# Moving streamed rows to other places modulo 512 bytes in an fp32 encoder layer

## The chip, the cores and the metric

The kernel runs on one core of a Trainium2 chip. The metric is the device time of one execution in microseconds; a kernel's time is the median of its runs.

## What is computed

One encoder layer with two independent inputs of 1024 tokens and width 1024, in fp32: a normalised input is projected; one part goes through a gated long convolution by Fourier transforms (Hyena), one through attention in a window of 128; both are gated, merged and added to the input; then a gated feed-forward part with 2816 hidden columns.

```python
h = rmsnorm(x, norm1_g)
proj = h @ w_in
u_h, q, k, v, g_h, g_a = jnp.split(proj, splits, axis=-1)
y_h = hyena_mixer(u_h, short_w, short_b, filt, hyena_bias)
y_a = window_attention(partial_rope(q, pos), partial_rope(k, pos), v, sink_logit)
merged = sigmoid(g_h) * (y_h @ w_up_hyena) + sigmoid(g_a) * (y_a @ w_up_attn)
x = x + merged @ w_out
h = rmsnorm(x, norm2_g)
x = x + (silu(h @ w_ff_gate) * (h @ w_ff_up)) @ w_ff_down
```

## The kernel before, in words

Activations lie with features on the 128 partitions and tokens along the row, so a tile of [128, 1024] fp32 is a row of 4096 bytes in each partition. To reach fp32 precision, each large product is made of three matmuls in the type fp32r: every operand is split into a high part (a cast on ScalarE) and a low rest (a subtraction on VectorE), and high x high, high x low and low x high are added up in PSUM. In each matmul one operand is loaded as weights (128 columns, 512 bytes a partition) and the other, the right-hand side, is streamed past it (mostly 512 columns, 2048 bytes).

The tiles that matter here:

- whi and wlo, split weights (pool wp, left side), loaded as weights in every large product but those for q, k and v.
- hh0 to hh7 and hl0 to hl7, the high and low rows of the normalised input (pool pa). They are streamed in the projections for the convolution (gemm_rows, L584 to L586) and for the gates (L570 to L572), and loaded as weights in the projection for q, k and v (L778 to L780, 256 columns streamed from whi and wlo). Those hl rows whose slots were taken before by x0, the raw input, lie with it.
- yh, yl and mh, ml, the split rows of the merge (pools ya and ma), streamed at L570 to L572 too.
- r, a ring of 28 tiles that hold a high and a low row each, streamed in the feed-forward part, which uses Strassen's scheme (L1061 to L1063 up, L1258 to L1260 down). 21 of them are in the pool ra on the right side of SBUF, 7 in the pool ff on the left. GpSimd's queue fills them from DRAM (sides_in, L1040).
- the right side also holds, at other times, the tiles of the filters, the convolution and the attention.

SBUF is handed out in units of 32 bytes from both sides: pools on the left in the order in which they are opened, those with side="right" from the top downward. Tiles of the large pools are multiples of 512 bytes, so the place of a pool modulo 512 is the place of all its rows, and column slices of 128 or 512 fp32 keep it. Three tiles called gap, which nothing reads, set these places: one of 120 fp32 at the top of the right side, one of 8 at the bottom of the left side, and one of 32 in the pool pb, below ya, ma and ff. With them all the rows named above begin at 0 modulo 512. Two tiles in pb, s and xin, begin at 384.

The order of instructions is the order in which the Python code is written, with convolution and attention mixed into the projections by a table of rates; each engine runs its own list, and waits on the others by semaphores.

Of the kernel before, what the change touches and what calls it, by code (L numbers as in the profile page):

```python
# [11 lines left out]
F32 = mybir.dt.float32  # L12
F32R = mybir.dt.float32r
# [6 lines left out]
P = 128  # L20
T = 1024
# [91 lines left out]
class Ops:  # L113
    def __init__(self, tc):
        self.tc = tc
        self.nc = tc.nc
# [101 lines left out]
class Kern:  # L218
    def __init__(self, ctx, tc, a):
        self.ctx, self.tc, self.nc, self.a = ctx, tc, tc.nc, a  # L220
        self.sm = ctx.enter_context(tc.tile_pool(name="sm", bufs=1, space=PSUM))
        self.dr = ctx.enter_context(tc.tile_pool(name="dr", bufs=1, space=DRAM))
        self.cp = cp = ctx.enter_context(tc.tile_pool(name="cp", bufs=1))
        edge = ctx.enter_context(tc.tile_pool(name="edge", bufs=1, side="right"))
        self.nc.vector.memset(edge.tile([P, 120], F32, name="gap"), 0.0)
        self.nc.vector.memset(cp.tile([P, 8], F32, name="gap"), 0.0)
        self.gn = cp.tile([P, 3, KC], F32, name="gn")
        self.sw = cp.tile([P, 4, 12], F32, name="sw")
        self.eps = cp.tile([P, 1], F32, name="eps")
        self.sink = cp.tile([P, NQ], F32, name="sink")  # L230
        self.ident = self.cp.tile([P, P], F32, name="ident")
        make_identity(self.nc, self.ident)
        self.rates = RATES
        self.sas = itertools.cycle(("sa", "sd"))
        self.full = set()

    def psm(self, tag="sa"):
        if tag == "sa":
            tag = next(self.sas)
        return self.sm.tile([P, 512], F32, tag=tag, name=tag)  # L240
# [400 lines left out]
            nc.vector.tensor_tensor(acc[:, s], acc[:, s], sq, ALU.add)  # L641

    def h_tiles(self, hp, k):
        return [hp.tile([P, T], F32R, tag=f"h{e}{k}", name=f"h{e}{k}", bufs=1) for e in "hl"]


    def norm_stats(self, pool, src):
# [55 lines left out]
            self.nc.sync.dma_start(self.hn[k], x)  # L703

    def next_rows(self, pool):
        hs = []
        ws = [self.weights(self.a["w_u"][j], 8, P) for j in range(2)]
        for k in range(KC):
            x = pool.tile([P, T], F32, tag="t4", name="xin")
            self.nc.sync.dma_start(x, self.hn[k])  # L710
            hi, lo = self.h_tiles(pool, k)
            for s in HALVES:
                self.part(hi[:, s], lo[:, s], x[:, s])
            hs.append((hi, lo))
        todo = [(w, s, self.pmm()) for w, s in ((ws[0], HALVES[0]), (ws[1], HALVES[0]), (ws[0], HALVES[1]))]
        for _ in self.gemm_rows(todo, hs):
            pass
        self.late = lambda: self.gemm_one(ws[1], hs, HALVES[1])
        return hs, [todo[0][2], todo[2][2], todo[1][2]]
# [591 lines left out]
    def main(self, outs):  # L1311
        nc, tc = self.nc, self.tc
        self.setup()

        def drain(g):
            for _ in g:
                pass

        def mix(main, side, rate):

            t = 0.0
            for c in main:
                t += c * rate
                while side is not None and t > 0:
                    d = next(side, None)
                    if d is None:
                        side = None
                    else:
                        t -= d
            return side  # L1330
# [6 lines left out]
        def slow(g, f):  # L1337
            for c in g:
                yield c * f

        def chain(*gs):
            for g in gs:
                if g is not None:
                    yield from g
# [4 lines left out]
        with tc.tile_pool(name="pa", bufs=PA, reuse_waits="tile") as pool:  # L1349
            hs, early = self.first_rows(pool, xT[0])  # L1350
# [6 lines left out]
            hs, early = self.next_rows(pool)  # L1357
# [5 lines left out]
        with tc.tile_pool(name="pb", bufs=TB, reuse_waits="tile") as tmp:  # L1363
            acc = [None, None]
            hb = [{}, {}]
            rr = [None, None]
            with tc.tile_pool(name="ya", bufs=1, reuse_waits="tile") as yp, tc.tile_pool(name="ma", bufs=1, reuse_waits="tile") as pool:
                mr, ms = {}, {}

                def hyena_up(u):  # L1370
                    mr[u] = [yp.tile([P, 512], F32, tag=f"x{j}", name=f"x{j}") for j in range(8)]
                    yield from self.merge_up(u // 2, 0, mr[u], None, yp, pool, tmp, HALVES[u % 2])

                def attn_up(u):
                    ms[u] = []
                    yield from self.merge_up(u // 2, 1, mr[u], ms[u], yp, pool, tmp, HALVES[u % 2])

                def outp(u):
                    if u % 2 == 0:
                        acc[u // 2] = tmp.tile([P, T], F32, tag="ar", name="acc", bufs=self.arb)  # L1380
                    yield from self.merge_out(u // 2, ms[u], tmp, acc[u // 2], HALVES[u % 2])

                side = mix(chain(hyena_up(0), attn_up(0), hyena_up(1), outp(0), attn_up(1), hyena_up(2), outp(1)), side, R[6])
                if side:
                    drain(side)
                self.ra = self.ctx.enter_context(tc.tile_pool(name="ra", bufs=1, side="right", reuse_waits="tile"))

                def start(s):
                    rr[s] = self.norm_scale(tmp, acc[s])

                def first_b():
                    start(0)
                    rr[0] = self.spread_dma(tmp, rr[0])
                    yield 8
                    for k in range(3):
                        yield from self.b_side(tmp, 0, k, rr[0], hb[0])
                    two = [tmp.tile([P, 512], F32R, tag=YR[0], name="b11", bufs=YR[1]) for _ in range(2)]
                    self.b3 = self.b_side(tmp, 0, 3, rr[0], hb[0], two)
                    yield next(self.b3)

                side = mix(chain(slow(attn_up(2), UPW), slow(hyena_up(3), UPW), outp(2), slow(attn_up(3), UPW), outp(3)), first_b(), R[7])
                if side:
                    drain(side)
            with tc.tile_pool(name="ff", bufs=1, reuse_waits="tile") as fp:
                self.fp = fp
                nc.vector.memset(tmp.tile([P, 32], F32, tag="gap", name="gap", bufs=1), 0.0)
                self.stages = itertools.cycle(range(3))
                self.turn = itertools.cycle((None, "sa", None, "sb", "sa", None, "sc"))
                drain(self.b3)
                front = [None, None]  # L1410

                def load_front(s, pairs):
                    front[s] = (pairs, self.plain_acts(s, pairs, self.ring_tiles()))

                def scale_1():
                    start(1)
                    rr[1] = self.spread_dma(tmp, rr[1])

                def side_1(k):
                    t = fp.tile([P, 2, 2, 512], F32, tag="x3", name="xin", bufs=1)  # L1420
                    self.scaled(1, k, rr[1], (t[:, 0], t[:, 1]))
                    self.sides_out(t[:, 0], t[:, 1], self.bs[k])

                def squares():
                    acc = tmp.tile([P, T], F32, tag="ar", name="acc", bufs=self.arb)
                    for j in range(8):
                        self.square_sum(tmp, acc, x1[j], j == 0)
                    self.rf = self.final_scale(acc, tmp, slice(0, T))

                hooks = {2 * k + 1: lambda k=k: side_1(k) for k in range(4)}  # L1430
                self.ffn_up(0, hb[0], tmp, {0: scale_1, **hooks}, lambda: load_front(0, (0, 1)))
                x1, hb[1] = self.ffn_down(0, front[0], tmp, None, lambda: self.sides_in(self.bs))
                self.ffn_up(1, hb[1], tmp, {0: squares, 1: lambda: drain(self.finish(x1, self.rf, outs[0], slice(0, T)))}, lambda: load_front(1, (0,)))
                self.ffn_down(1, front[1], tmp, outs[1], lambda: None)
# [55 lines left out]
```

## Time and profile before

| | |
|---|---|
| median of 3 runs | 2923.15 us (2921.74 to 2924.38) |
| the profiled execution | 2927.37 us, span 2925.6 us |
| granted TensorE clock, mean | 0.989 |
| instructions | 36421 |
| DMA | 510.90 MB, mean 175 GB/s |

The profile's page gives each engine's busy time and share of the span; the timeline gives the start and the duration of single instructions; groups by line give the count, the busy time, the mean duration and the idle time before them with what ended it. PE is TensorE, PEld its weight loads, DVE VectorE, ACT ScalarE, POOL GpSimd. The time from one matmul's start to the next one's is called a step below.

### The profile page before, as it was taken

Reading aid. Unit: us, or ns where it says so; the run is one execution under the profiler, and the core shown is the slowest. Engines: PE = TensorE matmul, PEld = TensorE weight load, DVE = VectorE, ACT = ScalarE, POOL = GpSimd, SP = SyncE. Lnnn points to the kernel's source line nnn. Section 1 sums busy time; section 2 is a strip of 40 time slices with the busy share of each in tenths; the row PEclk is TensorE's granted clock in tenths of the full one; section 3 lists DMA queues with packets and bytes.
Section 4 is the critical chain, followed back from the end, with each engine's and each line's share of the span. In section 5 each row is a group of like instructions: output and inputs, shape, how many; then the busy total and the mean of one; then the engine's idle time right before and its main releaser. Section 6 shows DMA issues by size and latency. Waiting matters only on the chain.

```text
span 2925.6 us, 36421 instructions
## 1 busy us (share of the span) xinstructions
PE 2850.6 (97%) x13498; PEld 2340.6 (80%) x13498; DVE 2113.9 (72%) x3440; ACT 1231.9 (42%) x2040; POOL 74.9 (3%) x146
## 2 busy tenths in 40 slices
PE   8999799999999999999999999999999999999998
PEld 6789687877798778778887788888888888888887
DVE  6876799887766886796587667776555767766566
ACT  5344322267722324895454434444112434443122
POOL 0000000000000000000000000000122000001200
PEclk9999899999999999999999999999999999999999
DMA  4454665432263433446766345556666334447641
GB/s 160 145 206 169 229 218 180 145 125 67 67 199 117 160 118 120 142 137 190 228 225 201 128 153 201 204 217 243 268 247 256 131 128 158 159 158 290 268 158 68
DMA packets 202429, 510.90 MB, mean 175 GB/s; under 512 B 19623, under 2 KB 68427, under 8 KB 202253
## 3 DMA queue, kind: packets, MB, share of 16 engines
q1 hardware_dynamic: 182093, 435.18, 43.4%
q0 software_dynamic: 20160, 73.41, 6.3%
q8 instruction: 106, 1.74, 0.2%
q14 instruction: 70, 0.57, 0.1%
HBM read 350.69 MB, written 157.83 MB: 174 GB/s over the span
## 4 chain that ended last, share of the span: by engine, by line
PE 82%; DVE 8%; DMA 5%; ACT 4%; issue 1%; SPq 0%; DVEq 0%; ACTq 0%
PE mm L570 7%; PE mm L571 7%; PE mm L572 7%; PE mm L1061 4%; PE mm L1062 4%; PE mm L1063 4%; PE sc L403 2%; DMA gin<-gt 2%; PE mm L1260 2%; PE mm L1259 2%; PE mm L1258 2%; PE sb L1061 1%; PE sb L1063 1%; PE sc L1062 1%; PE sb L1062 1%
## 5 line engine op out<-in xcount | busy, mean ns | idle before, releaser
L348 ACT CAST whi<-raw 128x1024 fp32r<-128x1024 f32 (+1 forms) x270 | 264.9, 981 | 582.6 <-PE mm L571 208.7
L349 DVE TENSOR_TENSOR wlo<-raw,whi 128x1024 fp32r<-128x1024 f32 (+1 forms) x270 | 306.2, 1135 | 203.5 <-ACT whi L348 203.0
L570 PE MATMUL mm<-hh,whi 128*128 128x512 f32 x824 | 334.2, 406 | 12.1 <-DVE ge L797 12.1
L571 PE MATMUL mm<-hl,whi 128*128 128x512 f32 x824 | 334.4, 406 | 0.0
L572 PE MATMUL mm<-hh,wlo 128*128 128x512 f32 x824 | 333.3, 405 | 0.0
L348 ACT CAST whi<-s 128x1024 fp32r<-128x1024 f32 x104 | 109.1, 1049 | 243.6 <-PE mm L1062 57.0
L1062 PE MATMUL mm<-r,whi 128*128 128x512 f32 x518 | 201.8, 390 | 0.0
L1061 PE MATMUL mm<-r,whi 128*128 128x512 f32 x518 | 201.8, 390 | 0.0
L1063 PE MATMUL mm<-r,wlo 128*128 128x512 f32 x518 | 201.6, 389 | 0.0
L570 PEld LDWEIGHTS mm<-hh,whi 128*128 128x128 f32 x824 | 155.6, 189 | 40.6 <-DVE ge L797 12.6
L572 PEld LDWEIGHTS mm<-hh,wlo 128*128 128x128 f32 x824 | 155.4, 189 | 28.7 <-issue 0.5
L571 PEld LDWEIGHTS mm<-hl,whi 128*128 128x128 f32 x824 | 155.7, 189 | 28.4 <-issue 0.7
L349 DVE TENSOR_TENSOR wlo<-s,whi 128x1024 fp32r<-128x1024 f32 x104 | 127.1, 1222 | 15.9 <-ACT whi L348 15.4
L1040 POOL DMA_DIRECT2D r<-comb x112 | 59.4, 530 | 2650.8 <-PE mm L1063 2034.9
L1061 PEld LDWEIGHTS mm<-r,whi 128*128 128x128 f32 x518 | 97.4, 188 | 20.9 <-ACT c L1122 0.4
L1063 PEld LDWEIGHTS mm<-r,wlo 128*128 128x128 f32 x518 | 97.4, 188 | 20.6 <-DVE wlo L349 0.3
L1062 PEld LDWEIGHTS mm<-r,whi 128*128 128x128 f32 x518 | 97.4, 188 | 20.2
L778 PE MATMUL mm<-whi,hh 128*128 128x256 f32 x384 | 112.1, 294 | 0.0
L779 PE MATMUL mm<-wlo,hh 128*128 128x256 f32 x384 | 111.7, 292 | 0.0
L780 PE MATMUL mm<-whi,hl 128*128 128x256 f32 x384 | 110.6, 288 | 0.0
L570 PE MATMUL mm<-yh,whi 128*128 128x512 f32 x256 | 102.1, 402 | 5.2 <-DVE gin L938 3.9
L571 PE MATMUL mm<-yl,whi 128*128 128x512 f32 x256 | 102.1, 401 | 1.0 <-DVE yl L349 1.0
(586 smaller groups left out, 7270.3 us busy)
## 6 DMA issues: line engine op xcount, KB each, us to landing
r<-comb POOLq DMA_DIRECT2D x112, 512.0 KB, 9.6
comb<-stage SPq DMA_DIRECT2D x48, 1024.0 KB, 5.0
K<-kd SPq DMA_DIRECT2D x64, 384.0 KB, 3.4
raw<-in_w_fg SPq DMA_DIRECT2D x44, 512.0 KB, 5.5
raw<-in_w_fu SPq DMA_DIRECT2D x44, 512.0 KB, 3.8
raw<-in_w_g SPq DMA_DIRECT2D x32, 512.0 KB, 4.0
gt<-ge SPq DMA_DIRECT2D x32, 512.0 KB, 2.6
raw<-in_w_up SPq DMA_DIRECT2D x32, 512.0 KB, 4.2
```

Source lines behind the costliest of these rows:

```text
L348: self.nc.scalar.copy(hi, src)
L349: self.nc.vector.tensor_tensor(lo, src, hi.bitcast(F32), ALU.subtract)
L570: mm(ps, hi[:, k], xh[:, s], start=(i == 0), stop=False)
L571: mm(ps, hi[:, k], xl[:, s], start=False, stop=False)
L572: mm(ps, lo[:, k], xh[:, s], start=False, stop=(i == n - 1))
L778: nc.tensor.matmul(ps[:, q], xh[:, t], wh, start=(i == 0), stop=False)
L779: nc.tensor.matmul(ps[:, q], xh[:, t], wl, start=False, stop=False)
L780: nc.tensor.matmul(ps[:, q], xl[:, t], wh, start=False, stop=(i == 7))
L1040: self.nc.gpsimd.dma_start(t.bitcast(F32), src[q][PLACE[name]])
L1061: mm(ps, hi[:, k], xh, start=(first and k == 0), stop=False, skip_group_check=not first)
L1062: mm(ps, hi[:, k], xl, start=False, stop=False, skip_group_check=not first)
L1063: mm(ps, lo[:, k], xh, start=False, stop=(k == n - 1), skip_group_check=not first)
```

## The change

The gap tile on the right shrinks from 480 to 416 bytes, the one in pb grows from 128 to 160, and after each of the first six pairs of h tiles stands a new gap tile of 32 bytes, in the first input's pass only (the second one uses the same slots).

```diff
-        self.nc.vector.memset(edge.tile([P, 120], F32, name="gap"), 0.0)
+        self.nc.vector.memset(edge.tile([P, 104], F32, name="gap"), 0.0)
         self.nc.vector.memset(cp.tile([P, 8], F32, name="gap"), 0.0)
...
+        self.pad = True
...
     def h_tiles(self, hp, k):
-        return [hp.tile([P, T], F32R, tag=f"h{e}{k}", name=f"h{e}{k}", bufs=1) for e in "hl"]
+        hs = [hp.tile([P, T], F32R, tag=f"h{e}{k}", name=f"h{e}{k}", bufs=1) for e in "hl"]
+        if self.pad and k < 6:
+            self.nc.vector.memset(hp.tile([P, 8], F32, tag=f"gap{k}", name="gap", bufs=1), 0.0)
+        return hs
...
     def next_rows(self, pool):
+        self.pad = False
...
-                nc.vector.memset(tmp.tile([P, 32], F32, tag="gap", name="gap", bufs=1), 0.0)
+                nc.vector.memset(tmp.tile([P, 40], F32, tag="gap", name="gap", bufs=1), 0.0)
```

Worked out from the allocation, the places modulo 512 bytes are:

| rows | before | after |
|---|---|---|
| weights whi, wlo | 0 | 0 |
| hl0 to hl7, hh0 | 0 | 0 |
| hh1, hh2, hh3, hh4, hh5, hh6, hh7 | 0 | 32, 64, 96, 128, 160, 192, 192 |
| yh, yl, mh, ml | 0 | 32 |
| r in ff (7 tiles), and the other tiles of ff | 0 | 32 |
| r in ra (21 tiles) | 0 | 64 |
| filters, convolution, attention (right side) | 0 | 64 |

On TensorE, ScalarE, GpSimd and SyncE the instructions and their order are the same as before. Only VectorE's list changes, at its start. These are its first rows before:

```order
L225 MEMSET gap 128x120
L226 MEMSET gap 128x8
L508 MEMSET onef 128x128
L518 MEMSET eps 128x1
L262 MEMSET w_490 66x128
```

and here the same place after the change:

```order
L225 MEMSET gap 128x104
L226 MEMSET gap 128x8
L509 MEMSET onef 128x128
L647 MEMSET gap 128x8 x6
L519 MEMSET eps 128x1
L263 MEMSET w_502 66x128
```

The six new memsets stand together behind that of onef, ahead of all arithmetic on VectorE; the code reaches them only with the rows' loop, but nothing holds them back.

## The prediction

> **What bounds the kernel now.** I read the page's busy line and chain first, to see which engine sets the end.
>
> ```profile
> span 2925.6 us, 36421 instructions
> PE 2850.6 (97%) x13498; PEld 2340.6 (80%) x13498; DVE 2113.9 (72%) x3440; ACT 1231.9 (42%) x2040; POOL 74.9 (3%) x146
> PE 82%; DVE 8%; DMA 5%; ACT 4%; issue 1%; SPq 0%; DVEq 0%; ACTq 0%
> ```
>
> TensorE is busy for 97% of the span and carries 82% of the chain that ends last. The ends of matmuls are modelled in this profile, so their durations (389 ns) overlap and say nothing of the rate. The rate is read from the starts in the timeline. In a quiet stretch of the gates' projection, 18 matmuls of 512 columns follow each other (first and last here):
>
> ```profile
> 561.01 0.39 PE L570 MATMUL mm<-hh,whi 128*128 128x512 f32 x1
> ...
> 564.86 0.39 PE L572 MATMUL mm<-hh,wlo 128*128 128x512 f32 x1
> ```
>
> That is 17 steps in 3.85 us, 226.5 ns each. The same reading for the 256-column form (14 rows, first and last):
>
> ```profile
> 257.07 0.28 PE L780 MATMUL mm<-whi,hl 128*128 128x256 f32 x1
> ...
> 258.63 0.28 PE L778 MATMUL mm<-whi,hh 128*128 128x256 f32 x1
> ```
>
> 13 steps in 1.56 us are 120 ns. So 256 more columns cost 106.5 ns, and of each step 226.5 - 2 x 106.5 = 13.5 ns is a fixed part that doesn't grow with the columns. In the kernel before, every operand of these matmuls, the streamed one and the weights, begins at 0 modulo 512 bytes. If the start addresses matter to TensorE, it is in these 13.5 ns, or in the slower steps where the stream is broken up.
>
> **The change part by part.** The programs have the same instructions in the same order on every engine, and every wait names the same semaphore; the counts waited for on VectorE are higher by six. What differs is addresses and memsets.
>
> *Six memsets of 128x8.* They stand on VectorE between the memset of onef and that of eps. Their price is that of the existing 128x8 memset, 0.07 us, so 6 x 0.07 = 0.4 us:
>
> ```profile
> 0.94 0.07 DVE L226 MEMSET gap<- 128x8 f32 x1
> 1.27 0.30 DVE L262 MEMSET wi<- 128x128 f32 x2
> 6.02 0.75 DVE L678 SCALAR_TENSOR_TENSOR hl<-x,gn,hh 128x512 fp32r<-128x512 f32 x1 [4.45 <-ACT hh L677]
> ```
>
> Behind them VectorE has nothing until 6.02 us, and sat idle for 4.45 us until ScalarE wrote hh from the first rows. 0.4 us lie inside that; queued behind are the memsets of eps, w and wi, which nobody needs in that time. Cost 0. With the cover gone it would be 0.4 us. The edge's memset is 16 columns shorter, which is hidden at the same place.
>
> *The memset in the second half grows from 32 to 40 columns:*
>
> ```profile
> L1406 DVE MEMSET gap<- x1: 85/85/85, 1184.6 to 1184.6; 128x32 f32 x1
> ```
>
> 32 columns take 85 ns and 8 columns 0.07 us above, so 8 more cost some 5 ns. One matmul waits for it. Cost 0.
>
> *ScalarE and VectorE at other addresses.* The trace has one natural comparison: the casts and subtractions that split weights read either raw, which begins at 0 modulo 512, or s, which begins at 384 in both kernels.
>
> ```profile
> L349 DVE TENSOR_TENSOR wlo<-raw,whi 128x1024 fp32r<-128x1024 f32 x226 | 275.9, 1221 | 95.5 <-ACT whi L348 95.0 <-DMA raw<-in_w_o 0.2
> L349 DVE TENSOR_TENSOR wlo<-s,whi 128x1024 fp32r<-128x1024 f32 x104 | 127.1, 1222 | 15.9 <-ACT whi L348 15.4
> ```
>
> 1221 against 1222 ns: a place of 384 against 0 costs VectorE 1 ns. 0 it is, for the 32 to 192 of the change too; these engines are also not the bound.
>
> *TensorE's streamed rows.* This term decides. Counted in the program, 8430 matmuls of 512 columns stream from a moved place while their weights stay at 0: 5310 from the ring r (64 or 32), 768 each from yh/yl and mh/ml (32), 1568 from hh1 to hh7 (32 to 192), 16 from one tile of the last down projection. The lows hl and hh0 stay at 0. No matmul of the kernel before has another relation than 0 to 0, so the cost must be bounded.
>
> The one thing the trace does vary is the time at which the next weights are loaded while a row streams. In the even stream the load starts with the matmul before it. Where the attention's work cuts in, it starts later, so the weight rows are read against another part of the streamed row:
>
> ```profile
> 1265.80 0.39 PE L570 MATMUL mm<-yh,whi 128*128 128x512 f32 x1
> 1265.80 0.19 PEld L571 LDWEIGHTS mm<-yl,whi 128*128 128x128 f32 x1
> 1266.03 0.39 PE L571 MATMUL mm<-yl,whi 128*128 128x512 f32 x1
> 1266.10 0.19 PEld L907 LDWEIGHTS sc<-ph,vv 128*128 128x128 f32 x1
> 1266.25 0.39 PE L907 MATMUL sc<-ph,vv 128*128 128x512 f32 x1
> ```
>
> ```profile
> 1227.12 0.39 PE L571 MATMUL mm<-yl,whi 128*128 128x512 f32 x1
> 1227.23 0.19 PEld L907 LDWEIGHTS sc<-ph,vv 128*128 128x128 f32 x1 [0.16 <-issue]
> 1227.35 0.39 PE L907 MATMUL sc<-ph,vv 128*128 128x512 f32 x1
> ```
>
> With the load at the start the step is 0.23 us; with the load 0.07 us late it is 0.22; 0.11 us late it is 0.23. At 106.5 ns for 256 columns of 4 bytes, 0.07 us is some 670 bytes of the streamed row: more than any offset of the change. If the fixed 13.5 ns came from the two reads meeting, a shift in time should have removed it as a shift of address would. It did not. So I take 0 for this term.
>
> TensorE's page in the Trainium skill ("TensorE: Matmul & The Clock Gate", section "Step-by-step: what each phase is for") says that the streamed operand and the weights are read through two independent ports. By that rule the address could not matter, and the sum would be 0; the two late loads above agree with it, though they shift time and not place.
>
> The far ends stand beside it. Downward: the fp32 matmuls of the convolution step in 0.43 us for two, 215 ns, the shortest step of a comparable length here; if all moved rows reached it, 8430 x (226.5 - 215) = 97 us are gained. Upward: right after a switch from those, the steps are longer.
>
> ```profile
> 566.39 0.58 PE L571 MATMUL mm<-hl,whi 128*128 128x512 f32 x1
> 566.81 0.40 PE L572 MATMUL mm<-hh,wlo 128*128 128x512 f32 x1
> 567.04 0.40 PE L570 MATMUL mm<-hh,whi 128*128 128x512 f32 x1
> 567.28 0.40 PE L571 MATMUL mm<-hl,whi 128*128 128x512 f32 x1
> 567.51 0.59 PE L407 MATMUL sd<-A,dft_f 128*128 128x256 f32 x2
> 567.94 0.59 PE L408 MATMUL sd<-A,dft_f 128*128 128x256 f32 x2
> 568.37 0.59 PE L403 MATMUL sc<-As,dft_f 128*128 128x256 f32 x2
> ```
>
> From 566.81 to 567.51 three steps take 0.70 us, 233 ns. Moved rows that never fell into the even step would lose 8430 x (233 - 226.5) = 55 us.
>
> The same page (section "Back-to-back issue gap") gives an isolated step of columns / 2.4 + 2.5 ns, which by estimate is 216 ns for 512 columns. The trace shows 226.5. If the difference were a matter of addresses, the estimate would put the gain at 8430 x 10.5 = 89 us; no row here ties it to addresses.
>
> *The sum.* 0 + 0 + 0 + 0. The profiled execution took 2927.37 us (span 2925.6), 4.2 us above the median of the runs, 2923.15; the sum is zero against either, so the forecast is the median, 2923.
>
> **The rivals.**
>
> *Faster: moved rows lose the fixed part.* For it: the fixed 13.5 ns is there in every step, and 0 against 0 is the one relation that the kernel has. The projections of the inputs also lose more than the ring does:
>
> ```profile
> L570 PE MATMUL mm<-hh,whi 128*128 128x512 f32 x824 | 334.2, 406 | 12.1 <-DVE ge L797 12.1
> L1258 PE MATMUL mm<-r,whi 128*128 128x512 f32 x196 | 76.2, 389 | 0.0
> ```
>
> 406 against 389 ns over 3 x 824 instructions is 42 us, though those rows also share TensorE with the convolutions. Against it: the late loads above. Half of the fixed gain, 97 / 2 = 48 us, would give 2875; all of it 2826.
>
> *Slower: the rows lose the even step.* The run of exactly repeating steps holds only with the streamed row and the weights at the same place; with rows at 32 k, three successive matmuls on hh, hl, hh start at three relations, and each step is like those after a switch. The price is up to 55 us (2978), half of it 28 us (2951). It decides from 1 ns a step on. For it: steps of 233 ns exist. Against it: those stand only behind fp32 matmuls, where the stream was broken.
>
> *Slower: transfers into moved rows.* The ring's fills write 4096-byte rows that would begin at 64 or 32.
>
> ```profile
> r<-comb POOLq DMA_DIRECT2D x112, 512.0 KB, 9.6
> POOL r L1040 <- PE mm L1063: 2034.9, 2, 2033.0
> POOL r L1040 <- DMA r<-comb: 37.9, 27, 2.5
> ```
>
> A sixteenth more on 9.6 us is 0.6 us for each of 140 fills (112 and 28), 84 us if none were hidden. But the fills wait for slots that TensorE frees (2033 us at once), and the list of TensorE's waits names no fill among its 22 longest; its longest is for VectorE. A fill stays hidden unless its landing grows by microseconds.
>
> ```profile
> PE mm L570 <- DVE ge L797: 12.1, 1, 12.1
> ```
>
> The DMA page of the Trainium skill ("DMA: Bandwidth & Descriptors", section "How a descriptor splits into AXI transactions") lets a row that doesn't begin at 256 bytes cost one more transaction, 17 for 16; that is where the sixteenth would come from. No row here shows it.
>
> **How the numbers follow.** A measurement of this kernel tells 0.2%, 5.8 us, from no change. No effect on TensorE, within 2917 to 2929: 0.43. Faster, by the fixed part or some of it: 0.33, spread from 2917 down to 2826, more of it near the small end, since the late loads speak against the whole. Slower through the uneven step: 0.21, from 2929 to 2978. Slower through transfers: 0.03. The likeliest single case is no effect, 2923. The range from 2868 to 2955 leaves out about a quarter of the faster case and a third of the slower one, 0.08 and 0.08.
>
> **What would show it.** In the changed kernel's timeline the step of quiet stretches tells all: 226.5 ns for r, yh, mh and hh1 to hh7 confirms the forecast; 215 to 224 means the faster rival, 228 or more the slower one. hl and hh0, which stay at 0, are the control within the same stretch, as is the 256-column form at 120 ns. If r<-comb lands later than 9.6 us, the transfers have changed. The prediction is wrong if places modulo 512 matter to TensorE in a way that a shift in time doesn't imitate: through the place of a row itself, or through that of the row streamed before it.

## The result and the profile after

The changed kernel takes 2948.85 us (median of 4 runs, 2943.69 to 2950.16) against 2923.77: a ratio of 1.0082, 95% interval [1.0064, 1.0099]. The difference of the medians is 25 us. The page of its profiled execution (2950.11 us) begins:

```profile
span 2948.3 us, 36427 instructions
PE 2881.2 (98%) x13498; PEld 2336.7 (79%) x13498; DVE 2115.3 (72%) x3446; ACT 1233.1 (42%) x2040; POOL 75.2 (3%) x146
PE 85%; DVE 6%; DMA 4%; ACT 4%; issue 1%; SPq 0%; DVEq 0%; ACTq 0%
```

The span is 22.7 us longer, TensorE is busy for 30.6 us more (its ends are modelled, so only the sign counts), and the chain has more of TensorE and less of VectorE in it. VectorE, ScalarE and GpSimd do what they did. The clock is not the cause: the granted clock is 0.991 on average for 0.989 before, and 1.00 in either trace from 1700 to 2000 us and from 2300 to 2800 us, deep in the feed-forward part.

Where the time lies is read from the first and the last start of the ring's matmuls, in the list of the instructions that read the tile r (count, then duration as minimum/median/maximum in ns, then first and last start in us). Before:

```profile
L1061 PE MATMUL mm<-r,whi x518: 387/389/628, 1618.5 to 2680.6; 128*128 128x512 f32 x173
L1260 PE MATMUL mm<-r,wlo x196: 389/389/389, 2092.6 to 2861.3; 128*128 128x512 f32 x196
```

and after:

```profile
L1066 PE MATMUL mm<-r,whi x518: 387/394/632, 1620.8 to 2699.8; 128*128 128x512 f32 x173
L1265 PE MATMUL mm<-r,wlo x196: 392/394/394, 2100.6 to 2883.5; 128*128 128x512 f32 x196
```

From 1618.5 to 2861.3 are 1242.8 us, from 1620.8 to 2883.5 are 1262.7: the feed-forward part is 19.9 us longer, and all that lies ahead of it only 2.3 us (a start that moves by some 4 us between traces whose steps are alike: 1614.7 us in the run further down that moves everything by 32 bytes).

The timeline shows how. In a quiet stretch of the down projection, 16 rows each, first and last, before:

```profile
2149.75 0.39 PE L1260 MATMUL mm<-r,wlo 128*128 128x512 f32 x1
...
2153.15 0.39 PE L1260 MATMUL sa<-r,wlo 128*128 128x512 f32 x1
```

and after:

```profile
2162.83 0.39 PE L1265 MATMUL sa<-r,wlo 128*128 128x512 f32 x1
...
2166.29 0.39 PE L1265 MATMUL mm<-r,wlo 128*128 128x512 f32 x1
```

15 steps took 3.40 us (226.7 ns each) and now take 3.46 (230.7). Over all steps of the ring shorter than 245 ns (5273 and 5282 of its 5310 rows in the two traces), the mean went from 226.8 to 230.8 ns: 5280 x 4.0 = 21 us, about the 19.9 us of that part. On the merge's rows, at 32, the step is longer still; 10 rows, first and last:

```profile
1454.70 0.40 PE L573 MATMUL mm<-mh,wlo 128*128 128x512 f32 x1
...
1456.80 0.39 PE L573 MATMUL mm<-mh,wlo 128*128 128x512 f32 x1
```

9 steps in 2.10 us are 233.3 ns.

### The profile page after: what moved, and what is told of

Its sections match the earlier page's. It is cut to its first block, busy times and chain, and to the rows that moved or that the text cites. A ratio compares the mean times of both kernels' runs of the same rounds, so it can differ in the third digit from the quotient of the medians.

```text
span 2948.3 us, 36427 instructions
## 1 busy us (share of the span) xinstructions
PE 2881.2 (98%) x13498; PEld 2336.7 (79%) x13498; DVE 2115.3 (72%) x3446; ACT 1233.1 (42%) x2040; POOL 75.2 (3%) x146
## 4 chain that ended last, share of the span: by engine, by line
PE 85%; DVE 6%; DMA 4%; ACT 4%; issue 1%; SPq 0%; DVEq 0%; ACTq 0%
PE mm L571 8%; PE mm L572 8%; PE mm L573 8%; PE mm L1066 4%; PE mm L1068 4%; PE mm L1067 4%; PE sc L404 2%; PE mm L1265 1%; PE mm L1263 1%; PE mm L1264 1%; PE sd L1066 1%; PE sb L1066 1%; PE sb L1068 1%; PE sb L1067 1%; PE sd L1068 1%; PE sd L1067 1%
```

## The experiments

The first theory is that a step depends on the relation of places: where the streamed row begins, modulo some length, against where the weights begin. Its rivals are the absolute place of the streamed row, the switching between successive rows of different places, and late transfers. "Mean step" below is the mean over the steps under 245 ns from the start of a row's matmul to the next matmul's start, worked out from the starts in each run's trace (5273 to 5293 steps for the ring). A ratio is taken against runs of the kernel before that were made beside the run.

### One part of the change at a time

**The right side alone.**

```diff
-        self.nc.vector.memset(edge.tile([P, 120], F32, name="gap"), 0.0)
+        self.nc.vector.memset(edge.tile([P, 104], F32, name="gap"), 0.0)
```

> Only the right side's gap tile is changed (to 416 bytes): the 21 ring tiles r in ra, with the tiles of convolution and attention, begin at 64; all else at 0 as before. Relation theory (a step is longer when the streamed row and the weights begin at different places): 4060 matmuls on those ring tiles lose 3 to 5 ns each, +12 to +20 us, 2936 to 2944; hh, yh and mh keep the 226.7 ns step. Transfers theory (the ring's fills into moved rows are late): the step stays 226.7 and waits for r appear on TensorE, with the same sum. Succession theory (what costs is that the place differs from one streamed row to the next): only the switches between ring tiles at 64 and at 0 are slow, a half of the four rows' groups, +6 to +10 us.

Measured: 2945.39 us, ratio 1.009 [1.0075, 1.0105]. This part alone brings the whole loss; 24 us is more than the relation theory (12 to 20) or the succession theory (6 to 10) had. In the timeline, 16 rows:

```profile
2162.70 0.40 PE L1260 MATMUL sc<-r,wlo 128*128 128x512 f32 x1
...
2166.20 0.39 PE L1260 MATMUL sa<-r,wlo 128*128 128x512 f32 x1
```

15 steps in 3.50 us, 233.3 ns. Over the trace, the ring's rows at 64 step in 231.7 ns and the seven tiles' rows that stayed at 0 in 232.6; hh, yh and mh, untouched, step as before (228.9, 229.0 and 227.0 ns). TensorE's list of waits names no transfer, and r<-comb lands in 9.3 us for 9.6: matmuls went slow without a wait, so it isn't the transfers. But a row at 0, whose weights are at 0, became slow too, because its neighbours moved: the relation of one row to its weights is not all.

**Without the gap tiles behind the h rows.** The change, with h_tiles as before.

> The change without the six gap tiles behind the h rows: hh0 to hh7 begin at 0, the ring at 64 and 32, yh and mh at 32. Relation theory: the gates' and convolution's projections go back to 226.7 ns in quiet stretches, some 3 ns for 2472 matmuls and 168 more, so 7 to 9 us less than the changed kernel: 2940 to 2942. Absolute-place theory says the same here. Succession theory: the graded rows are the worst part, 15 us less or more: 2934.

Measured: 2945.21 us, ratio 1.0088 [1.0071, 1.0105]. The mean step of hh goes back from 232.3 ns to 228.9, but the ratio can't be told from that of the whole change. The 15 us of the succession theory are excluded by the interval, and the 7 to 9 us of the relation theory did not show either. The projections' longer steps, 3.4 ns x 2330 = 8 us, hardly reach the end. From the kernel before to the changed one, ahead of the feed-forward part, the steps under 245 ns of the h, y and m rows add up to 20 us more, and their longer steps, which hold waits and switches to other matmuls, to 14 us less; which waits these are was not taken apart.

**Without the larger gap tile in pb.** The change, with the tile of 32 columns.

> The change without the larger gap tile in pb: yh, yl, mh, ml and the seven ring tiles in ff begin at 0, the ring in ra at 64, hh1 to hh7 at 32 to 192. Relation and absolute-place theories: mh and yh go back to 227 ns where they are even (5 to 7 us), and the ring's rows in ff gain some 3 ns for 1250 matmuls (4 us): 9 to 11 us less than the changed kernel, 2938 to 2940. Succession theory: the ring now switches between 64 and 0 in place of 64 and 32, so it gains nothing there, and mh, yh were uniform at 32 and can gain nothing: 2949.

Measured: 2950.03 us, ratio 1.0104 [1.0089, 1.0119]. Here the plain relation theory failed. mh and yh did go back (226.8 and 228.6 ns), but the ring lost as much: in its Strassen products, 64 beside 0 steps in 231.7 and 232.5 ns, 64 beside 32 (the change) in 230.6 and 230.9. Fewer rows moved, and no gain; 2949 was what the succession theory had for this run.

### Absolute place or relation

Everything is moved by 32 bytes, weights too.

```diff
-        self.nc.vector.memset(edge.tile([P, 120], F32, name="gap"), 0.0)
-        self.nc.vector.memset(cp.tile([P, 8], F32, name="gap"), 0.0)
+        self.nc.vector.memset(edge.tile([P, 112], F32, name="gap"), 0.0)
+        self.nc.vector.memset(cp.tile([P, 16], F32, name="gap"), 0.0)
```

> Everything in SBUF begins 32 bytes higher modulo 512, weights and streamed rows alike. Relation theory: 0 against 0 has become 32 against 32, the step stays 226.7 ns and the time is that before, 2924 within 0.2%. Absolute-place theory (a streamed row that doesn't begin at 512 costs): all 9936 matmuls of 512 columns take what mh took at 32 in the changed kernel, 234 ns in place of 227, +60 to +70 us, 2985 to 2994.

Measured: 2923.8 us, ratio 1.0012 [1.0003, 1.0022]. In the ring, 16 rows:

```profile
2149.82 0.39 PE L1258 MATMUL sa<-r,whi 128*128 128x512 f32 x1
...
2153.22 0.39 PE L1258 MATMUL sc<-r,whi 128*128 128x512 f32 x1
```

15 steps in 3.40 us, 226.7 ns: rows at 32 are as fast as rows at 0 when the weights are at 32. The absolute place is out, with the 60 to 70 us that it would have cost. A tenth of a per cent remains, inside what counts as no change here, and isn't in the steps (mean 226.8).

### The curve of the relation

The weights stay at 0, and all streamed rows, with the whole right side, begin at one other place u; nothing switches among the ring's rows. A pool that holds only a gap stands behind the weights' pool, and the edge shrinks by the same bytes. For 32:

```diff
-        self.nc.vector.memset(edge.tile([P, 120], F32, name="gap"), 0.0)
+        self.nc.vector.memset(edge.tile([P, 112], F32, name="gap"), 0.0)
...
         self.wp = ctx.enter_context(tc.tile_pool(name="wp", bufs=1))
+        after = ctx.enter_context(tc.tile_pool(name="after", bufs=1))
+        self.nc.vector.memset(after.tile([P, 8], F32, name="gap"), 0.0)
```

> Weights stay at 0, and all streamed rows (h, y, m, the whole ring, and the right side) begin at 32: one relation everywhere. If a step depends on the relation of row and weights alone, all 9936 matmuls of 512 columns take what mh took at 32, 233.4 ns: the ring's stages lose 5354 x 6.6 = 35 us, merges 1500 x 5 to 6 = 8 us, projections little (their longer steps hardly showed in the stage times): 2960 to 2975. If it is the switching between rows of different places that costs, nothing switches here: 2921 to 2927, step 226.7.

> The same with 64 for all streamed rows. Relation alone: the ring's rows take the 226, 229, 232 ns of three successive matmuls seen at 64 in the changed kernel (mean 229), +13 us on the ring, or the 233 to 234 also seen there, +36 us: 2936 to 2965. Switching alone: 2921 to 2927.

> The same with 128. If the relation counts modulo a short length (64 or 128 bytes), the step is 226.7 again and the time 2921 to 2927. If it counts modulo 256 or 512, the step is another than 226.7, between 226 and 237, 2921 to 2975.

> The same with 256. If the relation counts modulo 256 or less, the step is 226.7 and the time 2921 to 2927; if modulo 512, half a turn away is the largest distance and the step is as at 32 or longer, 2960 to 2990, or, if the even step at 0 was a standing conflict after all, shorter than 226 and the time under 2915.

> Weights at 0, all streamed rows at 96. The relation counts modulo 256 (256 gave the step of 0), so 96 is a point of its own. In the changed kernel rows at 96 stood between rows at 0 and showed 233 ns. Relation theory: one step for all rows, 229 to 234 ns, 2937 to 2965. If the relation were symmetric about 128, 96 would equal 160.

> The same with 160. Mean step in the changed kernel, between rows at 0: 234 ns. Relation theory: 229 to 234 ns, 2937 to 2965; symmetric about 128 (that is, only the distance counts): the step and time of 96.

> The same with 192. If only the distance modulo 256 counts, 192 is 64 on the other side: step 228.9 ns and 2933 to 2938 as at 64. If the direction counts (the stream runs ahead of the weight load rather than behind it), another step, perhaps under 226.7, which would beat both kernels.

> The same with 224. If only the distance modulo 256 counts, it is 32 on the other side: step 233.3 ns, 2960 to 2963 as at 32. If the direction counts, another step, perhaps under 226.7.

| place of rows, weights at 0 | time, us | ratio to before | mean step of the ring, ns |
|---|---|---|---|
| 0 (before) | 2923.15 | 1 | 226.8 |
| 32 | 2961.58 | 1.0133 [1.0118, 1.0149] | 233.3 |
| 64 | 2936.99 | 1.0046 [1.0031, 1.0062] | 228.9 |
| 96 | 2962.55 | 1.0139 [1.0123, 1.0154] | 233.3 |
| 128 | 2958.23 | 1.0119 [1.0098, 1.0140] | 232.7 |
| 160 | 2968.83 | 1.0159 [1.0142, 1.0176] | 234.3 |
| 192 | 2962.39 | 1.0138 [1.0123, 1.0153] | 233.3 |
| 224 | 2962.61 | 1.0137 [1.0122, 1.0152] | 233.3 |
| 256 | 2923.90 | 1.0002 [0.9992, 1.0012] | 226.8 |

Five of the kernels in the timeline of the down projection. At 32 (16 rows, 15 steps in 3.50 us, 233.3 ns):

```profile
2174.82 0.39 PE L1261 MATMUL sc<-r,whi 128*128 128x512 f32 x1
...
2178.32 0.40 PE L1261 MATMUL sa<-r,whi 128*128 128x512 f32 x1
```

At 64 (17 rows, 16 steps in 3.67 us, 229.4 ns):

```profile
2154.67 0.39 PE L1261 MATMUL mm<-r,whi 128*128 128x512 f32 x1
...
2158.34 0.39 PE L1262 MATMUL mm<-r,wlo 128*128 128x512 f32 x1
```

At 160 (16 rows, 15 steps in 3.51 us, 234.0 ns):

```profile
2174.78 0.39 PE L1262 MATMUL mm<-r,wlo 128*128 128x512 f32 x1
...
2178.29 0.39 PE L1262 MATMUL sc<-r,wlo 128*128 128x512 f32 x1
```

At 192 (16 rows, 15 steps in 3.50 us, 233.3 ns):

```profile
2174.71 0.40 PE L1260 MATMUL sc<-r,whi 128*128 128x512 f32 x1
...
2178.21 0.39 PE L1260 MATMUL mm<-r,whi 128*128 128x512 f32 x1
```

At 256 (17 rows, 16 steps in 3.63 us, 226.9 ns):

```profile
2149.74 0.39 PE L1260 MATMUL mm<-r,whi 128*128 128x512 f32 x1
...
2153.37 0.39 PE L1261 MATMUL sa<-r,whi 128*128 128x512 f32 x1
```

A uniform place of 32 costs 39 us, more than the change, so a loss needs no switching: the relation to the weights is a cause by itself. It counts modulo 256 bytes, not 512, as far as the one pair of 0 and 256 shows: half a turn of the 512 is no distance at all. It isn't a matter of distance alone, since 64 (228.9) and 192 (233.3) differ, though 32 and 224 are alike. And no place of the nine has a mean step of the ring under 226.8 ns, so none beats the kernel before. One time missed its expected range: 160 is 4 us above it.

The relation is not the whole of the change's loss. Three quarters of its ring lie at 64 and one quarter at 32, and the uniform steps give 0.75 x 2.1 + 0.25 x 6.5 = 3.2 ns of the 4.0; 0.8 are left to the mixed order. In the first experiment, with 64 and 0, they give 0.75 x 2.1 = 1.6 of 5.1, and the mixed order brings more than the relation. In the changed kernel's Strassen products the code takes three tiles in ra, then one in ff: the first step on each new place is 236.9 and 236.0 ns, and the steps on the second and third tile in ra have a mean of 229.2, close to the 228.9 of a uniform 64.

At 32 too, most of the sum reaches the end of the part. The list of r's instructions in that run:

```profile
L1063 PE MATMUL mm<-r,whi x518: 390/396/632, 1623.2 to 2710.4; 128*128 128x512 f32 x173
L1262 PE MATMUL mm<-r,wlo x196: 393/395/397, 2105.8 to 2896.1; 128*128 128x512 f32 x196
```

1272.9 us against 1242.8 before, 30 us more; 5290 x 6.5 = 34 us were due by the steps.

## Why the prediction was wrong, by its own steps

**The bound, the other engines, the memsets: right.** TensorE stayed the bound. The six memsets cost nothing; the one in pb, now 40 columns wide, takes 92 ns for 85.

```profile
L647 DVE MEMSET gap<- x6: 65/65/65, 1.1 to 1.2; 128x8 f32 x6
L1411 DVE MEMSET gap<- x1: 92/92/92, 1185.2 to 1185.2; 128x40 f32 x1
```

VectorE's split takes what it took, from either place, and the longest wait of TensorE is the same:

```profile
L350 DVE TENSOR_TENSOR wlo<-raw,whi 128x1024 fp32r<-128x1024 f32 x226 | 275.9, 1221 | 93.8 <-ACT whi L349 92.8 <-DMA raw<-in_w_o 0.5
L350 DVE TENSOR_TENSOR wlo<-s,whi 128x1024 fp32r<-128x1024 f32 x104 | 127.1, 1222 | 16.7 <-ACT whi L349 15.8
PE mm L571 <- DVE ge L802: 12.1, 1, 12.1
```

**The step that failed: "It did not. So I take 0 for this term."** The term of TensorE's streamed rows, put at 0, measured 4.0 ns a step on the ring (226.8 to 230.8), 21 us where the kernel lost 25. The late weight loads were asked only whether the fixed 13.5 ns goes away. Two of them were quoted, with steps of 0.22 and 0.23 us, at a resolution of 10 ns, although the prediction let the slower rival decide from 1 ns a step on. Worked out from the starts in that same trace, 29 loads in runs of 512-column matmuls start 26 to 134 ns late without a longer stop, and their steps have a mean of 230.7 ns, where 226.7 is the even one. So "It did not" holds for a shorter step and passed over a longer one.

That this mean is close to the changed kernel's 230.8 doesn't show that a shift in time stands for a shift of place. Of the 29 late loads, 21 stand where the attention cuts in, with a mean step of 231.4 ns; 45 loads that come on time at such a cut have 229.6 already, and the other 8 late ones have 228.9. A late load goes with some 2 ns. The prediction's last sentence had named this gap: places may matter in a way that a shift in time doesn't imitate. The runs show that the row's place relative to the weights matters, and so do the places of its neighbours; by what mechanism stays open.

**The rule on two independent ports** (the Trainium skill, "TensorE: Matmul & The Clock Gate", section "Step-by-step: what each phase is for") was taken to mean that an address couldn't matter. The measurement decides against that reading: with the same instructions and no new wait, the step depends on the place of the row relative to that of the weights. Whether the two reads meet in SBUF or elsewhere, no run here shows.

**The rivals.** The second one, rows that lose the even step, is what happened. Its price at half was 28 us, and 25 were measured; that they are close is luck, since the half was a fraction of 55 and not a count of rows. Its reason was half right: rows need the same place as the weights to keep the even step (32 against 32 keeps it, 32 against 0 doesn't). That graded places alone are the trouble was wrong, since one place of 32 for all rows is worse still. Its 55 us came from 233 ns for all 8430 rows; the ring got away with 230.8 because 64, the place of three quarters of it, is the mildest of the other places, and the projections' loss was mostly absorbed. The first rival's gain, a shorter fixed part, exists for the 512-column form at none of the nine places. Its 406 against 389 ns were modelled durations, which the prediction itself had set aside; by the starts, hh steps in 229.0 ns and the ring in 226.8. The transfers came as before (9.8 us for 9.6):

```profile
r<-comb POOLq DMA_DIRECT2D x112, 512.0 KB, 9.8
```

**The control that wasn't one.** hl and hh0 stayed at 0 and were to show 226.5 ns beside the moved rows. hl's mean step went from 228.9 to 232.2 ns with its neighbours, and the ring's unmoved tiles went slow in the first experiment. The other control, the 256-column form, moved as well, from 119.6 to 118.4 ns.

## What to carry to other kernels

Where TensorE is the bound, let every streamed row begin at the same place modulo 256 bytes as the weights that it meets (tried here: 0 with 0, 32 with 32, 256 with 0), and don't let the rows of a loop alternate between an even place and another; a small tile that shifts all rows by 32 bytes cost 1.3% here. Read the rate from the starts of successive matmuls: the modelled durations (389 ns) overlap and are not the step (226.8), though the ring's median durations moved by 3 to 7 ns here, about as much as the steps. When a trace offers a natural experiment for an effect of a few per cent, take the mean of all its cases at the trace's full resolution, and compare it with like cases without the effect; two hand-picked rows decide nothing.

## What was not expected of the hardware

- With fp32r matmuls of 512 columns, the mean step of the ring is 226.8 ns in the three pairs of places that agree modulo 256 bytes, and 228.9 to 234.3 ns at the seven other multiples of 32.
- The form with 256 columns goes the other way: its mean step, over some 1055 steps under 135 ns, is 119.6 ns before and at 256, 118.3 at 32, and 115.5 at 64, though 119.7 at 160. There the roles are swapped (the rows are the weights). That the 4 ns gained at 64 shorten the whole isn't shown: the feed-forward part starts no earlier there (1620.1 us for 1618.5).
- A mixed order can be worse than either of its places: rows at 64 and at 0 step in 231.7 and 232.6 ns beside each other, and in 228.9 and 226.8 among their like. It need not be: rows at 64 beside 32 step in 230.6 and 230.9, between the 228.9 and 233.3 of the two alone. Why the neighbour counts stays open.
